# An encoder on one core: the latents' second projections in the order queries, keys, values, and the last MLP group's squares and differences placed behind part of the down projection

## The chip, the cores and the metric

The kernel runs on one core of one Trainium2 chip. A core has five engines with a queue each: TensorE (PE) for matrix products, VectorE (DVE), ScalarE (ACT) and GpSimd (POOL) for work on elements, and SyncE (SP), which here does nothing but issue loads and stores. Each engine runs its queue in order and waits on semaphores for the others. The metric is the device time of one execution in microseconds. Three runs of the kernel before took 2659.59, 2660.11 and 2661.64 us; the median, 2660.11, is the time that is predicted against.

## The reference

Two layers, 1024 tokens, width 1024, all in fp32. Each layer runs four attention groups side by side on one input projection, adds their output projection to `x`, and then an MLP with a squared ReLU:

```python
for l in range(DEPTH):
    h = rms_norm(x, norm1_g[l])
    proj = h @ w_in[l]
    ...
    y_a = mla_mixer(a_cq, a_ckv, a_kr, mla_q_norm_g[l], mla_w_uq[l], mla_kv_norm_g[l],
                    mla_w_uk[l], mla_w_uv[l], cos32, sin32)
    ...
    mix = jnp.concatenate([rms_norm(y_a, out_g_mla[l]), y_b,
                           rms_norm(y_c, out_g_swa[l]), rms_norm(y_d, out_g_na[l])], axis=-1)
    x = x + mix @ w_out[l]
    h = rms_norm(x, norm2_g[l])
    x = x + jnp.square(jax.nn.relu(h @ w_up[l])) @ w_down[l]
return rms_norm(x, final_norm_g)
```

Group A (`mla_mixer`) makes its queries, keys and values out of latents, by a second projection:

```python
q = (rms_norm(cq, q_norm_g) @ w_uq).reshape(B, S, MLA_HEADS, MLA_NOPE_DIM + MLA_ROPE_DIM)
q = jnp.concatenate([q[..., :MLA_NOPE_DIM], apply_rope(q[..., MLA_NOPE_DIM:], cos, sin)], axis=-1)
c = rms_norm(ckv, kv_norm_g)
k_nope = (c @ w_uk).reshape(B, S, MLA_HEADS, MLA_NOPE_DIM)
v = (c @ w_uv).reshape(B, S, MLA_HEADS, MLA_V_DIM)
```

## The kernel before

**Products.** Data stand transposed in SBUF: 128 features on the partitions, 1024 tokens along a row, worked on in halves of 512. An fp32 operand is cut into a rounded part and the rest (`split`, L191: ACT copies the rounded part, L195, DVE or POOL subtracts it, L189), and a product is three passes over these parts (`passes`, L221 to L223). A product therefore waits for ACT's copy and for the subtraction: `far` is an operand of the activations (rest on DVE), `wh` and `wl` are the two parts of a weight (rest on POOL in most of the MLP).

**Attention.** `weave` interleaves the heads of one group with a generator of other work (`fill`). While group D runs (`attn_d`, L492), the fill is the rest of group C's projection and then `latent_up` (L740): it loads the parts of the query latent (rank 192, so one tile of 128 rows and one of 64, stored twice) and of the key and value latent (rank 128), each as rounded part and rest (`latp`), the row factors of the norms (`rq`, `rkv`), and makes, half by half, four kinds of result: values, keys without rotation (two tiles of two heads each), queries without rotation (two such tiles) and the rotated query part. Each result is scaled, split and stored to DRAM (`va`, `kan`, `qan`, `qar`); group A's heads load it later into stacks. Between D and A lies group C (`attn_c`), whose fill holds the sums of the output projection (`sum`, loaded from x).

**MLP.** Both products are done with a seven-product scheme on 2 by 2 blocks. `mlp_up` (L1226) runs 16 groups `q`; each gives four blocks of hidden units (`p1`, `b21`, `u3`, `u2`). A block is rectified and scaled on DVE (L1256), squared on ACT (L1258) and stored to `acts` (`keep`, L1262); four differences of the squared blocks (`differ`, L1311) are stored as well, since down needs them as operands: `acts[q, 1]` to `acts[q, 7]`.

`mlp_down` (L1442) runs four parts `j`, each over four groups of hidden units and seven products, in the order 1, 2, 6, 7, 4, 5, 3. Product `o` loads `acts[4 * j + k, o]` for k = 0 to 3 (`op`, L1464), splits them (`far`), and adds each result to `x`. Products 1, 6, 7 and 4 of a part use the same four PSUM banks `u`, so PE may start block m of product 7 only when DVE has done the add of block m of product 6. The combinations of down's weights (L1495 to L1497, `raw<-raw`) run on DVE too.

**The order.** Inside the MLP PE's order is that of the code (`manual_schedule`, L1188). DVE, ACT, POOL and SP are ordered by a list scheduler. `tc.issue_after(ins)` holds back what is written in it behind `ins`, on the engine of `ins` and nowhere else.

**The last group.** At the end of `mlp_up`, group 15 still has its rectifying, squares, stores and differences to do. They are left in `self.finish_up` (L1438) and done inside down: its first entry, which is `done4` and `done3` (L1298, L1307), behind the last rounding of product 1 of j = 0 (L1481); its second, `differ`, is written at j = 1 ahead of product 6 (L1499) and tied to nothing. The loop of product 2 and of the weights' combinations in j = 0 is tied behind `self.rectified` (L1489), the last rectify that was written, so here that of `u2`. Group 15's results are read by j = 3.

## Time and profile before

| | us |
|---|---|
| median of three runs (lowest, highest) | 2660.11 (2659.59, 2661.64) |
| the profiled execution | 2666.08 |
| its span, from the first to the last instruction | 2664.3 |
| PE busy in the span | 2529.8 |
| DVE busy | 1950.1 |
| ACT busy | 1442.6 |
| POOL busy | 1127.8 |

The mean granted PE clock of the profiled execution is 0.971 of full speed. In the profile an instruction is named by line, engine, operation and tiles, `out<-in`, with the tiles' names of the program and the buffers' numbers left out: `x<-u` is an add of a product in bank `u` to x, `ev<-ev` a difference or a sum in the hidden blocks' buffers, `far<-act,far` the rest of an activation operand, `wl<-raw,wh` the rest of a weight. What stands in brackets is the idle time of the engine ahead of an instruction and what ended it. A window gives, for a stretch of the span, each engine's busy time and number of instructions, the granted clock and the share of the DMA engines' time that was in use.

### The profile page before, as it was taken

The numbers are of one execution on the slowest core, as the hardware profiler recorded it, in microseconds if no ns is written. First come the engines' busy times: TensorE is split into PE (matmuls) and PEld (weight loads), VectorE is DVE, ScalarE is ACT, GpSimd is POOL, SyncE is SP. The second block draws the span as 40 slices with busy tenths as digits, with TensorE's granted clock in tenths as the row PEclk, the third lists the DMA queues.
The fourth block names the chain that finished last, engine by engine and source line by source line (L and its number), as shares of the span: only waits on it lengthen the run. The fifth ranks groups of instructions, "written<-read, shape, count | busy, mean of one in ns | idle before, by whom it ended". The sixth has DMA issues, their size and how long they took to land.

```text
span 2664.3 us, 37498 instructions
## 1 busy us (share of the span) xinstructions
PE 2529.8 (95%) x12320; PEld 2105.1 (79%) x12320; DVE 1950.1 (73%) x3403; ACT 1442.6 (54%) x2612; POOL 1127.8 (42%) x800
## 2 busy tenths in 40 slices
PE   8899988999999998999999999889999999999998
PEld 7678877887788886888877788777877888878886
DVE  6677767784986668887568777677849866688876
ACT  4577756663644444444436777666735444444445
POOL 2465633211055554454425656332011555555554
PEclk9889998999999999999998999989999999999999
DMA  5634598331244456444245445963221544664431
GB/s 167 181 89 127 145 266 252 106 92 36 76 162 150 152 189 240 145 140 143 93 120 150 117 134 145 291 199 90 84 71 32 187 154 150 228 215 149 129 119 64
DMA packets 191539, 385.00 MB, mean 145 GB/s; under 512 B 23712, under 2 KB 34928, under 8 KB 191344
## 3 DMA queue, kind: packets, MB, share of 16 engines
q1 hardware_dynamic: 176976, 356.90, 44.2%
q10 hardware_dynamic: 14368, 25.70, 2.8%
q8 instruction: 98, 1.61, 0.3%
q14 instruction: 97, 0.79, 0.1%
HBM read 261.20 MB, written 121.32 MB: 144 GB/s over the span
## 4 chain that ended last, share of the span: by engine, by line
PE 73%; DVE 11%; DMA 7%; ACT 4%; issue 3%; POOL 1%; SPq 1%; DVEq 0%; POOLq 0%; ACTq 0%
PE u L221 8%; PE u L223 8%; PE u L222 8%; PE mm L221 5%; PE p L223 5%; PE p L221 5%; PE p L222 5%; PE mm L222 5%; PE mm L223 5%; PE sb L856 3%; DVE p L858 3%; PE tr L892 2%; DVE part L189 2%; ACT p L861 1%; PE pv L881 1%
## 5 line engine op out<-in xcount | busy, mean ns | idle before, releaser
L189 POOL TENSOR_TENSOR wl<-raw,wh 128x512 fp32r<-128x512 f32 x424 | 605.6, 1430 | 698.9 <-ACT wh L195 675.0
L195 ACT ACTIVATE wh<-raw 128x512 fp32r<-128x512 f32 x448 | 281.3, 629 | 578.3 <-PE u L222 311.4
L189 POOL TENSOR_TENSOR wl<-ws,wh 128x512 fp32r<-128x512 f32 (+1 forms) x120 | 151.1, 1261 | 451.1 <-ACT wh L195 444.2
L221 PE MATMUL u<-far,wh 128*128 128x512 f32 x768 | 301.1, 392 | 11.4 <-DVE x L189 9.2
L223 PE MATMUL u<-far,wl 128*128 128x512 f32 x768 | 300.9, 392 | 6.7 <-POOL wl L189 6.7
L222 PE MATMUL u<-far,wh 128*128 128x512 f32 x768 | 300.7, 392 | 0.0
L189 DVE TENSOR_TENSOR raw<-raw 128x512 f32<-128x512 f32 x256 | 224.9, 886 | 79.4 <-DMA raw<-in_w_up 43.1
L189 DVE TENSOR_TENSOR ptl<-tr,pth 128x512 fp32r<-128x512 f32 (+2 forms) x384 | 237.8, 628 | 60.5 <-ACT pth L195 59.4
L861 ACT ACTIVATE p<-p,nm 128x1024 f32<-128x1024 f32 x192 | 220.1, 1147 | 79.0 <-DVE nm L858 77.2
L195 ACT ACTIVATE pth<-tr 128x512 fp32r<-128x512 f32 (+2 forms) x384 | 206.0, 547 | 99.7 <-PE tr L892 63.6
L223 PE MATMUL p<-far,wl 128*128 128x512 f32 (+1 forms) x648 | 251.0, 387 | 4.0 <-DVE wl L189 4.0
L221 PE MATMUL p<-far,wh 128*128 128x512 f32 (+1 forms) x648 | 251.3, 388 | 0.0
L222 PE MATMUL p<-far,wh 128*128 128x512 f32 (+1 forms) x648 | 250.9, 387 | 0.0
L856 PE MATMUL sb<-stack 96*128 96x512 f32 x640 | 223.2, 430 | 13.9 <-DVE nm L858 12.9
L189 DVE TENSOR_TENSOR far<-act,far 128x512 fp32r<-128x512 f32 x224 | 206.1, 949 | 14.6 <-ACT far L195 14.6
L189 POOL TENSOR_TENSOR p<-p 128x1024 f32<-128x1024 f32 x64 | 154.8, 2419 | 106.3 <-ACT p L944 99.5
L221 PEld LDWEIGHTS u<-far,wh 128*128 128x128 f32 x768 | 145.1, 189 | 43.3 <-issue 10.0
L223 PEld LDWEIGHTS u<-far,wl 128*128 128x128 f32 x768 | 145.3, 189 | 37.9 <-POOL wl L189 7.8
L222 PEld LDWEIGHTS u<-far,wh 128*128 128x128 f32 x768 | 145.2, 189 | 31.0 <-DVE far L189 0.8
L221 PE MATMUL mm<-xh,wh 128*128 128x512 f32 x416 | 166.8, 401 | 1.8 <-DVE part L189 1.6
L892 PE MATMUL tr<-ident,p 128*128 128x128 f32 x1024 | 162.1, 280 | 6.3 <-DVE ptl L189 5.4
L858 DVE CUSTOM_DVE_ANT_0 p<-sb,zero 128x512 f32<-128x512 f32 x192 | 129.3, 685 | 49.5 <-PE sb L856 22.1
(255 smaller groups left out, 6150.7 us busy)
## 6 DMA issues: line engine op xcount, KB each, us to landing
act<-acts SPq DMA_DIRECT2D x224, 256.0 KB
raw<-in_w_up SPq DMA_DIRECT2D x128, 256.0 KB
acts<-ev SPq DMA_DIRECT2D x128, 256.0 KB
raw<-in_w_down SPq DMA_DIRECT2D x128, 256.0 KB
acts<-ev ACTq DMA_DIRECT2D x96, 256.0 KB
ws<-in_w_in SPq DMA_DIRECT2D x76, 256.0 KB
rz<-drows SPq DMA_DIRECT2D x40, 256.0 KB
stack<-kd SPq DMA_DIRECT2D x32, 256.0 KB
```

What stands on the lines that cost most here:

```text
L189: return (eng or self.nc.vector).tensor_tensor(out=out, in0=a, in1=b, op=op)
L195: self.rounded = nc.scalar.activation(hi, src, AF.Copy)
L221: mm(ps, w[0], x[0][:, sl], start=start, stop=False)
L222: mm(ps, w[0], x[1][:, sl], start=False, stop=False)
L223: mm(ps, w[1], x[0][:, sl], start=False, stop=stop)
L856: self.nc.tensor.matmul(ps, q[:, qt * P:(qt + 1) * P], k[:, sl], start=i == 0, stop=i == len(passes) - 1)
L858: self.nc.vector.tensor_tensor_reduce(out=p[:, sl], in0=ps, in1=self.zero[:, 0:1].bitcast(F).broadcast_to([P, 512]), scale=-scale, scalar= ...
L861: self.nc.scalar.activation(p, p, AF.Exp, bias=nm[:, 1:2], scale=-1.0, accum_out=z)
L881: nc.tensor.matmul(out, v[:, kt], lo[:, sl], start=False, stop=kt == 7)
L892: nc.tensor.transpose(t[:, k * 256 + i * P:k * 256 + (i + 1) * P], p[:, (j * 2 + k) * P:(j * 2 + k + 1) * P], self.ident)
```

## The change

Two functions' order changes; what is computed stays the same.

In `latent_up` the loads and the projections change places. The row factors are loaded first, then the query latents, then the key and value latent. The projections run: rotated queries, queries of the first two heads, keys of the first two heads, values, queries of the last two, keys of the last two. Before they ran: values, keys, queries of the last two heads, rotated queries, queries of the first two.

In the MLP the last group's work is parted otherwise. Behind product 1's rounding in j = 0 stand only the rectify of `b21`, which frees its bank, and the add to `u2`, which frees the other. The square and the store of `b21`, the rectifies, squares and stores of `u3` and `u2`, and `differ` stand at j = 1 and are tied behind the last add of j = 1's product 1. `self.rectified` is thereby `b21`'s rectify when j = 0's loop is tied to it.

```diff
@@ latent_up
-        def latent(i, r):
+        rq, rkv = self.big_tile(F, "rq"), self.big_tile(F, "rkv")
+        self.spread(rq, rows[0])
+        self.spread(rkv, rows[1])
+        parts = []
+        for i, r in ((0, P), (1, 64), (2, P)):
             p = []
             for j in range(2):
                 t = self.big_tile(R, "latp")
                 for at in range(0, P, r):
                     self.load(t.bitcast(F)[at:at + r], lat[j, i, :r])
                 p.append(t)
-            return tuple(p)
-
-        rkv = self.big_tile(F, "rkv")
-        kv = latent(2, P)
-        self.spread(rkv, rows[1])
-        q = [latent(0, P), latent(1, 64)]
-        rq = self.big_tile(F, "rq")
-        self.spread(rq, rows[0])
+            parts.append(tuple(p))
...
+        w0 = self.weights(d["w_lat"][l, 0])
+        yield from two([w0[0], both(w0[1])], parts[0:2], self.ev_rope(tabs, qr))
         plain = lambda r, dst: self.ev_plain(r, self.to_parts(dst))
+        yield from two([w0[2], both(w0[3])], parts[0:2], plain(rq, qn[:, 0]))
+        w1 = self.weights(d["w_lat"][l, 1])
+        yield from two(w1[2:3], parts[2:3], plain(rkv, kn[:, 0]))
         w2 = self.weights(d["w_lat"][l, 2])
         for t in range(2):
-            yield from two(w2[t:t + 1], [kv], self.ev_plain(rkv, self.to_values(va[2 * t:2 * t + 2])))
-        w1 = self.weights(d["w_lat"][l, 1])
-        for t in range(2):
-            yield from two(w1[2 + t:3 + t], [kv], plain(rkv, kn[:, t]))
-        yield from two([w1[0], both(w1[1])], q, plain(rq, qn[:, 1]))
-        w0 = self.weights(d["w_lat"][l, 0])
-        yield from two([w0[0], both(w0[1])], q, self.ev_rope(tabs, qr))
-        yield from two([w0[2], both(w0[3])], q, plain(rq, qn[:, 0]))
+            yield from two(w2[t:t + 1], parts[2:3], self.ev_plain(rkv, self.to_values(va[2 * t:2 * t + 2])))
+        yield from two([w1[0], both(w1[1])], parts[0:2], plain(rq, qn[:, 1]))
+        yield from two(w1[3:4], parts[2:3], plain(rkv, kn[:, 1]))
@@ mlp_up
             def relu2(v, src, n):
 
+                rectify(v, src, n)
+                nc.scalar.activation(v, v, AF.Square)
+                return v
+
+            def rectify(v, src, n):
                 self.rectified = nc.vector.scalar_tensor_tensor(out=v, in0=src, scalar=0.0, in1=rb[:, N[n]],
                                                                 op0=ALU.max, op1=ALU.mult)
-                nc.scalar.activation(v, v, AF.Square)
-                return v
...
-            self.finish_up = [lambda: (done4(s), done3(s)), lambda: differ(s)]
+
+            def free():
+                s.b21 = tmp()
+                rectify(s.b21, s.u, 0)
+                self.tt(s.u2, s.p, s.u2, ALU.add)
+
+            def rest():
+                nc.scalar.activation(s.b21, s.b21, AF.Square)
+                keep(s.q, 2, s.b21)
+                relu2(s.u3, s.u3, 1)
+                keep(s.q, 3, s.u3)
+                relu2(s.u2, s.u2, 1)
+                differ(s)
+
+            self.finish_up = [free, rest]
@@ mlp_down
-                self.tt(o, ps, o, ALU.add)
+                return self.tt(o, ps, o, ALU.add)
...
-                        add(m, 0, u[m])
+                        added = add(m, 0, u[m])
...
                 if j == 1:
-                    self.finish_up[1]()
+                    with tc.issue_after(added.ins):
+                        self.finish_up[1]()
```

How the orders differ, at three places. On DVE, layer 0, at the passage from up into down, the program before runs as follows, from the eight operand rests of product 1 of j = 0 onwards:

```order
L189 TENSOR_TENSOR far<-act,far 128x512 x8
L1256 SCALAR_TENSOR_TENSOR ev<-ev,rb 128x512
L1256 SCALAR_TENSOR_TENSOR ev<-u,rb 128x512
L189 TENSOR_TENSOR ev<-p,ev 128x512
L189 TENSOR_TENSOR far<-act,far 128x512
L1256 SCALAR_TENSOR_TENSOR ev<-ev,rb 128x512
L189 TENSOR_TENSOR raw<-raw 128x512 x4
L189 TENSOR_TENSOR far<-act,far 128x512 x3
```

and the changed program, at the same place:

```order
L189 TENSOR_TENSOR far<-act,far 128x512 x8
L1258 SCALAR_TENSOR_TENSOR ev<-u,rb 128x512
L189 TENSOR_TENSOR raw<-raw 128x512 x4
L189 TENSOR_TENSOR ev<-p,ev 128x512
L189 TENSOR_TENSOR raw<-raw 128x512
L189 TENSOR_TENSOR far<-act,far 128x512
```

The two rectifies `ev<-ev,rb` (of u3 and u2) are gone from here, and the weights' combinations `raw<-raw` follow the first rectify at once. A little later, still in j = 0, the program before has the four differences among the adds of product 1 and the operands of products 6 and 7; here the last of product 1's adds with its neighbours:

```order
L189 TENSOR_TENSOR x_7183<-u,x_7183 128x512
L189 TENSOR_TENSOR far<-act,far 128x512
L189 TENSOR_TENSOR raw<-raw 128x512
L189 TENSOR_TENSOR far<-act,far 128x512
L189 TENSOR_TENSOR ev<-ev 128x512 x2
L189 TENSOR_TENSOR x_7190<-u,x_7190 128x512
```

and the changed program:

```order
L189 TENSOR_TENSOR x_7183<-u,x_7183 128x512
L189 TENSOR_TENSOR far<-act,far 128x512
L189 TENSOR_TENSOR raw<-raw 128x512
L189 TENSOR_TENSOR far<-act,far 128x512
L189 TENSOR_TENSOR x_7190<-u,x_7190 128x512
L189 TENSOR_TENSOR far<-act,far 128x512 x2
```

No difference `ev<-ev` is left in j = 0. In j = 1, on DVE as well, the changed program has them behind the last add of product 1:

```order
L189 TENSOR_TENSOR x_7190<-u,x_7190 128x512
L1258 SCALAR_TENSOR_TENSOR ev<-ev,rb 128x512 x2
L189 TENSOR_TENSOR far<-act,far 128x512 x2
L189 TENSOR_TENSOR raw<-raw 128x512
L189 TENSOR_TENSOR x_7169<-p,x_7169 128x512
L189 TENSOR_TENSOR ev<-ev 128x512
L189 TENSOR_TENSOR raw<-raw 128x512
L189 TENSOR_TENSOR x_7176<-p,x_7176 128x512
L189 TENSOR_TENSOR ev<-ev 128x512 x3
L189 TENSOR_TENSOR x_7183<-p,x_7183 128x512
```

The two rectifies stand ahead of the last two operand rests of product 6, the differences among the adds of product 2. On SP, layer 0, around `latent_up`'s loads (a piece of the difference, - before, + changed; `bias` and `kd` belong to group D, `in_w_lat` are the second projections' weights):

```order
 L160 DMA rz<-drows 64x1024
 L160 DMA v<-vd 128x1024
-L160 DMA latp<-lat 128x1024 x2
+L160 DMA rq<-drows 128x1024
 L160 DMA rkv<-drows 128x1024
 L160 DMA latp<-lat 128x1024 x2
 L160 DMA latp<-lat 64x1024 x4
-L160 DMA rq<-drows 128x1024
+L160 DMA latp<-lat 128x1024 x2
 L160 DMA ws<-in_w_out 128x256
 L160 DMA stack<-kd 64x1024 x2
 L160 DMA stack<-kc 64x1024
```

The first latent load stands behind two loads of row factors of 512 KB now; what comes after the group is as it was, the load of `bias` at its row included. Further on, the four loads `sum<-in_x` stand behind the first eight stack loads of group A, where before they stood ahead of all but one of them.

## The prediction

> **What bounds the kernel now.** I read the page's busy times and its chain first, then the table of windows, the waits of PE inside the windows that are not full, and last the timelines of DVE, PE and POOL there.
>
> ```profile
> PE 2529.8 (95%) x12320; PEld 2105.1 (79%) x12320; DVE 1950.1 (73%) x3403; ACT 1442.6 (54%) x2612; POOL 1127.8 (42%) x800
> PE 73%; DVE 11%; DMA 7%; ACT 4%; issue 3%; POOL 1%; SPq 1%; DVEq 0%; POOLq 0%; ACTq 0%
> ```
>
> PE bounds nearly everything: only 2664.3 − 2529.8 = 134.5 us of the span are without a matmul. The change leaves the number and kind of matmuls alone, so it can only move those 134.5 us and what PE loses at a lower clock. The windows show where (window, length, then busy time of PE, PEld, DVE, ACT and POOL with counts, granted PE clock, DMA share, GB/s):
>
> ```profile
> 356.00:400.00 44.00, 35.73 (x202) 30.68 (x200) 28.42 (x73) 26.40 (x69) 11.63 (x10) 0.92 0.98 280
> 1000.00:1060.00 60.00, 49.05 (x203) 38.83 (x202) 56.32 (x69) 28.16 (x50) 26.50 (x17) 0.92 0.68 236
> 1060.00:1335.00 275.00, 275.00 (x1215) 227.73 (x1214) 196.19 (x238) 121.37 (x194) 136.13 (x100) 1.00 0.42 134
> 1670.00:1700.00 30.00, 26.30 (x159) 23.15 (x157) 16.75 (x40) 16.83 (x41) 9.09 (x5) 0.94 1.04 291
> 2310.00:2370.00 60.00, 52.87 (x220) 42.71 (x219) 50.32 (x64) 30.42 (x53) 32.10 (x18) 0.91 0.77 267
> ```
>
> The rest of down (1060 to 1335) has no idle PE at all. The two passages from up into down (1000 to 1060 in layer 0, 2310 to 2370 in layer 1) lose 10.95 and 7.13 us, DVE being busy 56.32 of 60 us in the first. The two stretches in which `latent_up` runs (356 to 400, 1670 to 1700) lose 8.27 and 3.70 us, with the DMA engines full. So the change touches four places that lose about 30 us together; nothing else can pay.
>
> The waits of PE in the two passages (what waits, for whom: total, times, longest):
>
> ```profile
> PE u L221 <- DVE x L189: 9.2, 2, 7.6
> PE u L223 <- POOL wl L189: 0.6, 1, 0.6
> ...
> PE u L223 <- POOL wl L189: 6.0, 1, 6.0
> ```
>
> The first two rows are layer 0, the last is layer 1. They are different cases: layer 0 waits for DVE, layer 1 for one POOL operation.
>
> **Part 1: the last group's operations, layer 0.** DVE in the passage (start, duration, line, operation, count; the number in brackets, where there is one, is idle time before it), then PE around the long wait:
>
> ```profile
> 1012.94 1.77 DVE L1256 SCALAR_TENSOR_TENSOR ev<-ev,rb 128x512 f32<-128x512 f32 x1
> 1016.43 0.68 DVE L1256 SCALAR_TENSOR_TENSOR ev<-ev,rb 128x512 f32<-128x512 f32 x1
> 1030.37 0.68 DVE L189 TENSOR_TENSOR far<-act,far 128x512 fp32r<-128x512 f32 x1
> 1030.97 0.68 DVE L189 TENSOR_TENSOR x<-u,x 128x512 f32<-128x512 f32 x1
> 1032.77 0.68 DVE L189 TENSOR_TENSOR ev<-ev 128x512 f32<-128x512 f32 x1
> 1040.64 3.48 DVE L189 TENSOR_TENSOR ev<-ev 128x512 f32<-128x512 f32 x2
> 1048.73 1.75 DVE L189 TENSOR_TENSOR ev<-ev 128x512 f32<-128x512 f32 x1
> 1054.61 1.87 DVE L189 TENSOR_TENSOR x<-u,x 128x512 f32<-128x512 f32 x3
> ...
> 1047.46 0.39 PE L223 MATMUL u<-far,wl 128*128 128x512 f32 x1
> 1055.43 0.77 PE L221 MATMUL u<-far,wh 128*128 128x512 f32 x1 [7.58 <-DVE x L189]
> 1055.99 0.63 PE L222 MATMUL u<-far,wh 128*128 128x512 f32 x1
> 1060.24 0.40 PE L223 MATMUL u<-far,wl 128*128 128x512 f32 x1
> ```
>
> From 1012.94 DVE runs without a gap until the first of three adds at 1054.61, and that add (done about 1055.3) lets PE start product 7 at 1055.43. The six operations in the five rows of L1256 and ev<-ev are those that the change takes out of this stretch: two rectifies and four differences. All others stay, among them the rectify of b21 and the add ev<-p.
>
> As recorded the six take 1.77 + 0.68 + 0.68 + 3.48 + 1.75 = 8.36 us. That is not what removing them must give. The rows at 1030.37 and 1030.97 show operations following each other every 0.60 us; others take 1.7. The window from 1012.94 to the add's end says why:
>
> ```profile
> 1012.94:1055.28 42.34, 32.62 (x141) 25.66 (x139) 42.34 (x51) 20.00 (x35) 20.58 (x13) 0.94 0.54 179
> 1038.40 5.17 POOL L189 TENSOR_TENSOR wl<-raw,wh 128x512 fp32r<-128x512 f32 x3 [0.54 <-ACT wh L195]
> ```
>
> By the timeline 49 DVE operations begin in it and end by 1055.3 (the 51 adds one cut at either edge). 49 at 0.60 are 29.4 us; the 12.9 us over them match the 13 POOL operations at about 1.0 each (the row of three shows their length, 1.7): DVE and POOL take turns, and each turn of POOL costs whichever DVE operation is next. The POOL operations all stay. So 43 operations and 13 turns take 25.8 + 12.9 = 38.7 us, a gain of **6 × 0.60 = 3.6 us**; the upper end is 8.4 as recorded. I take 3.6, since all 13 turns remain and only their partners change.
>
> The Trainium skill bears on this choice: "SBUF — State Buffer", section "SBUF: two separate sides", says that VectorE with two SBUF inputs and GpSimd share one pair of ports as an exclusive lock held for a whole instruction. By that rule a removed instruction that had waited hands its wait to the next one, which gives the 3.6; were the long durations the instructions' own, the sum would be 8.4. The rows at 0.60 and 1.7 for one shape agree with the rule.
>
> What is late next: PE ended product 6 at 1047.46 + 0.39 = 1047.85, with two shorter waits before it (9.2 − 7.6 = 1.6 for DVE, 0.6 for POOL), so it can be ready at 1045.6 if those go. DVE's add comes at 1055.4 − 3.6 = 1051.8. A wait of about 6 us stays, as does the slow start behind it: from 1055.99 to 1060.24 ten matmuls come every 0.43 us, against 0.23 before (1047.46 and its neighbours), which costs 12 × 0.2 = 2.4 us. Layer 0 gains **3.6**.
>
> ACT: one square now sits among the copies of product 6's operands, two later ones are gone from there; at 0.6 us each beside an ACT busy 28.16 of 60 us they cost nothing; uncovered, 0.6. SP's four stores of the differences leave the queue of the operand loads, which then wait for nothing but their own buffers: nothing below zero counted. POOL's own queue is not changed.
>
> **Layer 1.** POOL at the place of the 6.0 us wait, DVE's operation that ends it, and PE:
>
> ```profile
> 2340.28 10.71 POOL L189 TENSOR_TENSOR wl<-raw,wh 128x512 fp32r<-128x512 f32 x3 [5.17 <-ACT wh L195]
> ...
> 2346.41 0.68 DVE L189 TENSOR_TENSOR x<-u,x 128x512 f32<-128x512 f32 x1
> 2372.43 1.87 DVE L189 TENSOR_TENSOR x<-u,x 128x512 f32<-128x512 f32 x3
> ...
> 2347.67 0.79 PE L223 MATMUL u<-far,wl 128*128 128x512 f32 x1 [6.04 <-POOL wl L189]
> 2353.80 0.43 PE L222 MATMUL p<-far,wh 128*128 128x512 f32 x1
> 2375.43 0.39 PE L221 MATMUL u<-far,wh 128*128 128x512 f32 x1
> ```
>
> Here one POOL operation, begun at 2340.28, ended only when DVE came to an add that reads PSUM at 2346.41; until then DVE's operations followed each other unhindered. PE lost 6.0 us, then 15 matmuls at 0.43 (up to 2353.80) another 3.0. It began product 7 at 2375.43 with no wait for DVE, whose add was done at 2373.05. If POOL is held up in the same way again, fewer DVE operations later help nobody: gain 0. If not, PE is ready at 2375.4 − 9.0 = 2366.4, and DVE, which now gives way to about three more POOL turns at 1.0 and has six operations fewer at 0.60, at 2373.05 + 3.0 − 3.6 = 2372.4; a wait of 6.0 and a slow start of 2.4 follow, and the matmuls behind it stand at 2374.9: gain 0.5. I take **0** for layer 1. The upper end is 8.4: the same six at recorded lengths (6.2) and no hold-up, 2375.4 less 2367.0. A new hold-up in layer 0 would cost 9.0 there, bring PE to product 7 at 1054.6 and remove the wait for DVE and its slow start: still 3.2 gained.
>
> **Where the six go: second part, j = 1.** DVE ahead of its product 6 and 7, and PE's first matmul of product 6:
>
> ```profile
> 1117.99 0.68 DVE L189 TENSOR_TENSOR raw<-raw 128x512 f32<-128x512 f32 x1
> 1126.17 0.68 DVE L189 TENSOR_TENSOR x<-u,x 128x512 f32<-128x512 f32 x1
> ...
> 1123.05 0.39 PE L221 MATMUL u<-far,wh 128*128 128x512 f32 x1
> ```
>
> Two rectifies now stand ahead of the last two operand pieces of product 6, which were ready at 1117.99, 5.1 us before PE wanted them; at 0.60 to 1.7 each they cost 1.2 to 3.4. All six stand ahead of product 7's last piece, ready at 1126.2; PE begins product 7 48 matmuls after 1123.05, at about 1134.0, so 7.8 us are free against 3.6 to 10.2. Cost **0** in both layers (nearest row: the mean of the six as recorded, 1.4, makes 8.4, of which only 0.6 would show, and that in the last piece); uncovered, 2.4 a layer. Behind the tied operations on DVE queue only these operands and adds. The three squares and six stores that land here meet a PE without idle time and DMA engines 42% busy; the stores are wanted by j = 3.
>
> **Part 2: `latent_up`.** No instruction is added or removed, so the price is one of order alone. PE at the first latent product and at the next long wait, DVE's wait behind that, then the sums:
>
> ```profile
> 367.94 0.47 PE L221 MATMUL mm<-latp,wh 128*128 128x512 f32 x1 [2.24 <-DMA latp<-lat]
> 369.13 0.50 PE L222 MATMUL mm<-latp,wh 128*128 128x512 f32 x1 [0.72 <-DMA latp<-lat]
> 387.72 1.62 PE L1026 MATMUL sb<-stack 128*128 128x384 f32 x4 [4.05 <-DVE nb L1102]
> DVE p L1102 <- DMA bias<-in_bias: 4.5, 1, 4.5
> 448.98 1.29 DVE L189 TENSOR_TENSOR sum<-mm,sum 128x512 f32<-128x512 f32 x2 [3.59 <-DMA sum<-in_x]
> PE sb L1026 <- DVE nb L1133: 4.5, 1, 4.5
> PE sb L1026 <- DVE nb L1133: 1.8, 1, 1.8
> ```
>
> The first product already waits for its loads, and two loads of 512 KB (rq, rkv) now stand ahead of them on SP. The two halves landed 1.2 us apart (367.94, 369.13), so the first product comes 2.4 later. It is now a query product, which also needs the four 256 KB loads behind: by the same pace another 2.4, of which the other matmuls that the order puts between hide some. PE is then 2.4 to 4.8 late; but at 387.72 it waited 4.05 for the bias load, which stands at the same row of SP behind the same bytes, so it lands as before and swallows about as much. Net 0 in layer 0; uncovered 4.8. Layer 1 has no such later load in its trace; the window from 1670 has 3.7 idle in all. Its ends are 0 and 4.8.
>
> The sums (loads of x for the output product) are issued behind the first stacks of group A rather than ahead, and DVE's adds stand later too. In before, DVE waited 3.6 for one and kept PE waiting 4.5 (layer 0), and 1.8 at the like place in layer 1. Ends: minus 6.3 if the later adds no longer wait, plus the like if the loads slip further than the adds. With costs of both signs and nearly equal ends I take **0** for all of attention.
>
> **Sum.** 3.6 + 0 + 0 + 0. The profiled execution took 2666.08, 6 us over the median 2660.11 of the runs; a difference of 3.6 (0.14%) carries over unchanged: 2660.1 − 3.6 = **2656.5**. About 0.2%, 5.3 us, is what a measurement here can tell from no change, so the forecast itself is on the edge of "same".
>
> **Rivals.**
> - Recorded lengths count (17%): the six take their 8.4 with them in layer 0. Then DVE's add comes at 1047.0, PE waits 1.4 instead of 7.6, and the slow start goes too: 8.4 + 2.4 = 10.8, 2649.3. For: 8.36 stood in the trace. Against: the sum of 0.60s and turns fits without them. The trace has no slow start behind the 1.6 us wait and one behind 6.0 and 7.6, so a short rest would spare the 2.4. The Trainium skill, "TensorE: Matmul & The Clock Gate", "What's actually happening", puts that limit at an idle window of about 3.4 us; by it the wait of 6 that I leave stays above, as the rows have it.
> - The sums stop blocking DVE (17%): 3.6 + 4.5 + 1.8 = 9.9, 2650.2. For: the adds stand later. Against: so do the loads.
> - Slower, the latents come late (20%): the 4.8 of the query product shows in both layers, 9.6 − 3.6 = +6.0, 2666.1. It decides once PE's delay exceeds the 4.05 of the bias wait, or if SP, waiting for PE to free stack buffers, issues the bias that much later. For: DMA shares of 0.98 and 1.04 there. Against: the cover in layer 0, and in layer 1 a DMA queue that PE did not wait for as long.
> - The moved work is not hidden (8%): 2.4 a layer in j = 1 gives back 4.8: 2661.3. Against: 7.8 us of room.
> - It does not do what it says (10%): layer 0 finds another last wait, POOL or a load, and stays at 2660.
>
> **Chances.** The forecast holds 28%, with its own range 2653 to 2659, of which a quarter (7%) lies under 2654.8. Faster: 17 + 17 + 7 = 41%. Slower: 20%. Within 0.2%: 21 + 8 + 10 = 39%. The range reaches from under the two fast rivals to over the slow one, 2646 to 2667; both fast ones together (2643) and 4.8 uncovered with j = 1 on top stay outside.
>
> **What would show it.** In the profile after: DVE's first add of product 6 in j = 0 some 38.7 us after its first rectify; a wait for DVE of about 6 us ahead of product 7 and ten matmuls at 0.43 behind it; in layer 1 either the same hold-up of POOL or a wait for DVE in its place; no idle PE in j = 1; the first latent matmul near 370, and the wait for the bias shorter by what that one grew. Wrong would be: a wait ahead of product 7 under 3 us, idle PE after 1060, or windows of `latent_up` more than 2 us longer or shorter.

## The result, and the profile after

The changed kernel takes 2643.61 us (median of six runs, 2638.36 to 2649.87); before, taken in the same session, 2658.05 (six runs, 2653.90 to 2661.64). The ratio is 0.9946, with a 95% interval of 0.9928 to 0.9963: 14.4 us faster, where 3.6 had been forecast, and outside the range. The profiled execution took 2649.87, its span is 2648.1; it is the longest of the six, and stands 16.2 below the profiled one of before, which at 2666.08 is itself longer than each of the six timed ones. So two profiles show where the time went, and the timings how much.

The busy times and the chain of the page of after:

```profile
PE 2524.9 (95%) x12320; PEld 2097.0 (79%) x12320; DVE 1950.6 (74%) x3403; ACT 1443.9 (55%) x2612; POOL 1134.4 (43%) x800
PE 74%; DVE 10%; DMA 6%; ACT 4%; issue 3%; POOL 2%; SPq 1%; DVEq 0%; POOLq 0%; ACTq 0%
```

The counts are those of before. PE is busy 4.9 us less (the same matmuls, at a mean granted clock of 0.975 instead of 0.971) and idle 11.3 less: 2648.1 − 2524.9 = 123.2 against 134.5.

To see where, I cut the executions at the same counts of matmuls. From the 1700th to the 2350th the kernels run the same matmuls in another order, and from the 7400th to the 8450th the same but for four. Cuts inside these two stretches don't part equal work, because the order differs. Counting the columns of each matmul (512 for a 128x512), those from 8000 to 8450 have 137,616 before and 131,600 after, and those from 7800 to 8000 have 54,048 and 57,248; in layer 0, from 1950 to 2350, the two kernels are within 0.4%. Stage lengths in us, from one profiled execution each:

| stage (cut at PE's matmuls) | before | after | after, profiled again |
|---|---|---|---|
| layer 0, latents and C, no. 1700 to 3400 | 334.8 | 328.8 | 324.7 |
| of which D gives way to C, 1950 to 2350 | 90.1 | 85.4 | 80.9 |
| layer 0, 1700 to 2350 (the same matmuls) | 142.8 | 136.4 | 132.6 |
| layer 0, passage up to down (420 matmuls) | 109.9 | 105.9 | 104.6 |
| layer 1, latents and C, 7800 to 9530 | 342.2 | 337.1 | 331.7 |
| of which the first latent products, 7800 to 8000 | 40.2 | 44.1 | 40.9 |
| of which D gives way to C, 8000 to 8450 | 102.9 | 94.7 | 92.9 |
| layer 1, 7400 to 8450 (the same but for four) | 217.7 | 213.7 | 208.6 |
| layer 1, passage up to down (420 matmuls) | 105.9 | 105.1 | 105.7 |

The two executions of the changed kernel differ by up to 5.4 us in a row, and those of another kernel below (the latents alone) by 10 in the first row, so single us mean nothing here. Still, against this one profile of before the attention gives 11 to 21 us, the MLP about 5. Part of that belongs to this profile: three kernels below that have the old `latent_up` as well take 332.2 to 334.3 us in the first row and 338.3 to 340.1 in layer 1's. I call the 400 matmuls (layer 0) and 450 (layer 1) in which group D's last heads, the last latent projections and group C's first heads mix **the turn**. Its windows, before (columns as in the prediction: PE, PEld, DVE, ACT, POOL, granted clock, DMA share, GB/s):

```profile
410.65:500.74 90.09, 75.73 (x401) 64.61 (x400) 66.24 (x165) 57.80 (x145) 32.40 (x29) 0.91 0.67 194
1711.20:1814.13 102.93, 88.37 (x452) 74.52 (x451) 76.64 (x194) 67.92 (x177) 37.44 (x33) 0.88 0.72 205
```

and after, with two windows of down behind product 6 of j = 0:

```profile
406.91:492.28 85.37, 75.28 (x402) 61.71 (x401) 62.75 (x162) 56.30 (x144) 24.55 (x25) 0.94 0.69 208
1704.44:1799.11 94.67, 83.05 (x452) 69.13 (x451) 72.63 (x186) 66.98 (x171) 28.25 (x27) 0.93 0.72 216
1040.00:1310.00 270.00, 270.00 (x1193) 223.65 (x1192) 195.94 (x241) 114.62 (x189) 134.45 (x100) 1.00 0.42 135
2350.00:2620.00 270.00, 270.00 (x1193) 223.65 (x1192) 204.83 (x253) 126.81 (x212) 135.71 (x99) 1.00 0.40 125
```

PE is idle in layer 0's turn for 10.1 us instead of 14.4, and in layer 1's for 11.6 instead of 14.6. There PE is also busy for 83.1 us instead of 88.4, but with 4.4% fewer columns, so most of that difference is work that now stands ahead of the cut. On the same matmuls layer 1 gains 4.0 and 9.1 us in the two profiles, not the 8.3 and 10.0 of the turn. In down PE is busy for every one of 540 us: the work that was moved into j = 1 is hidden.

What stood in the turn before, on DVE. Three of its groups by line in the first 44 us of layer 0's (count, busy time, mean ns of one, idle time ahead of them and what ended it):

```profile
L189 DVE TENSOR_TENSOR part<-mm,tabs 64x512 f32<-64x512 f32 x4 | 2.8, 689 | 0.1
L189 DVE TENSOR_TENSOR part<-mm,rq 128x512 f32<-128x512 f32 x3 | 2.1, 685 | 1.5 <-PE tr L1035 1.2 <-POOL both L189 0.3
L189 DVE TENSOR_TENSOR part<-mm,tabc 128x512 f32<-128x512 f32 x2 | 1.4, 681 | 0.0
```

Two rows of layer 1's timeline:

```profile
1720.38 0.69 DVE L189 TENSOR_TENSOR part<-mm,rq 128x512 f32<-128x512 f32 x1 [3.56 <-POOL both L189]
1723.17 0.68 DVE L189 TENSOR_TENSOR part<-mm,tabc 128x512 f32<-128x512 f32 x1
```

And DVE's two longest waits in the first 70 us of layer 1's turn (in total, times, longest):

```profile
DVE p L1133 <- PE tr L1035: 3.9, 2, 2.6
DVE part L189 <- POOL both L189: 3.6, 1, 3.6
```

The tabs and tabc rows are the rotated queries: three DVE and two POOL operations (`part`, `both`) for each half, all in the turn. In layer 1 DVE could not start a query's evacuation for 3.56 us, because POOL had not finished with an earlier one, and group D's and C's softmax stood in the same queue. In layer 0 the same wait is 0.3 us (the second row above), so it is not what layer 0 gained by. In after the rows of tabs and tabc are gone from both turns, and so is the wait; there stand, beside a query and a key projection, the values, whose evacuation has no POOL operation.

The passages: waits of PE, after, in layer 0 and then in layer 1:

```profile
PE u L223 <- POOL wl L189: 6.1, 1, 6.1
PE u L221 <- ACT ev L1292: 1.2, 1, 1.2
...
PE u L223 <- POOL wl L189: 6.7, 1, 6.7
PE u L221 <- ACT ev L1292: 1.1, 1, 1.1
```

and the timeline of POOL, DVE and PE in layer 0's:

```profile
1011.43 11.20 POOL L189 TENSOR_TENSOR wl<-raw,wh 128x512 fp32r<-128x512 f32 x3 [4.69 <-ACT wh L195]
1016.83 1.29 DVE L189 TENSOR_TENSOR far<-act,far 128x512 fp32r<-128x512 f32 x2
1018.04 0.69 DVE L189 TENSOR_TENSOR x<-u,x 128x512 f32<-128x512 f32 x1
1019.30 0.80 PE L223 MATMUL u<-far,wl 128*128 128x512 f32 x1 [6.05 <-POOL wl L189]
1024.59 0.63 PE L223 MATMUL p<-far,wl 128*128 128x512 f32 x1
1040.97 0.69 DVE L189 TENSOR_TENSOR x<-u,x 128x512 f32<-128x512 f32 x1 [1.84 <-PE u L223]
```

Layer 0 now has the hold-up that only layer 1 had: POOL's first operation begins at 1011.43 and alone takes 7.82 us, DVE's follow each other every 0.60 us, and POOL gets through when DVE comes to an add that reads PSUM, at 1018.04. PE waits 6.05 and then runs 12 matmuls at 0.43. In return it no longer waits 7.58 for DVE ahead of product 7; at 1040.97 DVE waits for PE.

### The profile page after: what moved, and what is told of

Read it like the earlier page. It is cut to its first block, busy times and chain, and to the rows that moved or that the text cites. A ratio compares the mean times of both kernels' runs of the same rounds, so it can differ in the third digit from the quotient of the medians.

```text
span 2648.1 us, 37521 instructions
## 1 busy us (share of the span) xinstructions
PE 2524.9 (95%) x12320; PEld 2097.0 (79%) x12320; DVE 1950.6 (74%) x3403; ACT 1443.9 (55%) x2612; POOL 1134.4 (43%) x800
## 4 chain that ended last, share of the span: by engine, by line
PE 74%; DVE 10%; DMA 6%; ACT 4%; issue 3%; POOL 2%; SPq 1%; DVEq 0%; POOLq 0%; ACTq 0%
PE u L221 9%; PE u L223 9%; PE u L222 8%; PE p L223 5%; PE p L221 5%; PE p L222 5%; PE mm L221 5%; PE mm L222 5%; PE mm L223 5%; PE sb L853 3%; PE tr L889 2%; DVE p L855 2%; DVE part L189 2%; DMA bias<-in_bias 2%; ACT p L858 1%
## 5 line engine op out<-in xcount | busy, mean ns | idle before, releaser
L189 POOL TENSOR_TENSOR wl<-raw,wh 128x512 fp32r<-128x512 f32 x424 | 611.9, 1444 | 688.9 <-ACT wh L195 671.4
L195 ACT ACTIVATE pth<-tr 128x512 fp32r<-128x512 f32 (+2 forms) x384 | 206.9, 548 | 100.5 <-PE tr L889 68.4
L853 PE MATMUL sb<-stack 96*128 96x512 f32 x640 | 220.0, 426 | 15.7 <-DVE nm L855 15.1
L223 PEld LDWEIGHTS u<-far,wl 128*128 128x128 f32 x768 | 145.1, 189 | 43.7 <-POOL wl L189 13.6
```

What stands on the lines that cost most here:

```text
L189: return (eng or self.nc.vector).tensor_tensor(out=out, in0=a, in1=b, op=op)
L195: self.rounded = nc.scalar.activation(hi, src, AF.Copy)
L223: mm(ps, w[1], x[0][:, sl], start=False, stop=stop)
L853: self.nc.tensor.matmul(ps, q[:, qt * P:(qt + 1) * P], k[:, sl], start=i == 0, stop=i == len(passes) - 1)
```

## The experiments

All ratios are against the kernel before on the same chip, with their 95% intervals. "Turn" gives the lengths between the same counts of matmuls as above, layer 0 and layer 1. Since these cuts don't part equal work in layer 1, here are for all profiles the two stretches that do, in us (in layer 1 at most five of the 1050 matmuls differ):

| kernel | layer 0, 1700 to 2350 | layer 1, 7400 to 8450 |
|---|---|---|
| old `latent_up`: before; MLP alone; differences alone; adds, old `latent_up` | 142.8; 142.8; 140.6; 140.7 | 217.7; 214.2; 216.3; 215.3 |
| new `latent_up`, both parts changed (two profiles) | 136.4; 132.6 | 213.7; 208.6 |
| new `latent_up`, the latents alone (two profiles) | 136.7; 129.3 | 205.8; 205.8 |
| new `latent_up` with the adds (two profiles) | 132.7; 131.8 | 203.0; 206.7 |
| new projections, old loads | 137.5 | 215.9 |
| rotated queries last | 143.5 | 212.9 |
| rotated queries first, the rest in the old order | 137.8 | 216.7 |
| values last; the same with the adds | 142.3; 141.6 | 216.3; 216.2 |
| factors first | 145.1 | 219.4 |
| POOL's operations on DVE | 146.3 | 219.6 |

**Each half alone.** `latent_up` changed and the MLP as before; then the MLP changed and `latent_up` as before.

> Only latent_up is changed; the MLP is as before. Theory A (the larger part of the gain is attention's: set against each other by the number of the matmul, the two profiles part by 6.4 us in layer 0 and by about 4 us in layer 1 between the start of latent_up and the end of group C): 8 to 12 us under the kernel before. Theory M (the gain is the MLP's, and attention's part of it is chance of the two profiled executions): within 3 us. Both: the passages from up into down are as before, 7.6 us of waiting for DVE in layer 0 and 6.0 for POOL in layer 1.

> Only the MLP is changed; latent_up is as before. Theory A: 4 to 6 us under the kernel before (4.1 in layer 0 and 0.9 in layer 1 by the two profiles), with a wait of about 6 us for one POOL operation in both layers and no wait for DVE. Theory M: 11 to 15 us.

The latents alone: 2649.62, 0.9946 [0.9926, 0.9965]; a second time 2647.07, 0.9948 [0.9931, 0.9966]. The MLP alone: 2654.85, 0.9977 [0.9965, 0.9990], which is 6.1 us with ends of 2.7 and 9.3. The turn in the first two executions of the latents alone:

```profile
410.13:494.26 84.13, 74.25 (x402) 61.97 (x401) 63.23 (x162) 56.36 (x144) 24.84 (x25) 0.94 0.71 211
1710.66:1799.41 88.75, 79.75 (x453) 64.97 (x451) 74.70 (x189) 66.64 (x174) 28.26 (x27) 0.98 0.77 234
```

```profile
403.03:483.31 80.28, 71.37 (x402) 59.00 (x401) 63.34 (x162) 56.22 (x144) 24.98 (x25) 0.98 0.71 221
1693.60:1784.44 90.84, 82.13 (x452) 67.77 (x451) 75.57 (x189) 66.98 (x174) 28.25 (x27) 0.94 0.76 230
```

So the part that I priced at nothing is worth about 14 us by the ratios (11.5 and 14.5 by the medians), and is there in both layers of both profiles. The code of the MLP is that of before here, but its passages are not: 110.0 and 109.4 us, the second time 109.4 and 110.9, against 109.9 and 105.9 before. PE's wait for DVE in layer 0's and layer 1's:

```profile
PE u L221 <- DVE x L189: 9.2, 1, 9.2
...
PE u L221 <- DVE x L189: 9.1, 1, 9.1
```

Beside the changed latents, then, the MLP's part gives 3.5 to 5.8 us in each layer's passage (105.9, 104.6 and 105.1, 105.7 in the changed kernel); beside the old ones it gives 3.7 and 1.1.

PE's waits in the two passages of the MLP alone:

```profile
PE u L221 <- DVE x L189: 5.5, 1, 5.5
PE u L221 <- ACT ev L1295: 1.1, 1, 1.1
PE u L221 <- ACT wh L195: 0.8, 1, 0.8
```

These three rows are the same in both layers. This is the forecast's own picture, a wait for DVE of about 6 with slow matmuls behind it (12 and 5), and no hold-up of POOL. In layer 0 DVE is done with the add that ends the wait 38.2 us after it began the first rectify; 38.7 had been forecast. Passages 106.2 and 104.9.

**Only the differences moved.** Before, with `differ` tied behind j = 1's add of product 1, and nothing else.

```diff
-                        add(m, 0, u[m])
+                        added = add(m, 0, u[m])
...
-                    self.finish_up[1]()
+                    with tc.issue_after(added.ins):
+                        self.finish_up[1]()
```

> The kernel before, with the four differences alone tied behind the add of j = 1; rectifies, squares and latent_up as before. At 0.60 an operation DVE's add ahead of product 7 in layer 0 comes 2.4 us earlier, at recorded lengths 5.9, which would end the slow matmuls as well (8). By the first, 2 to 3 us under the kernel before; by the second 6 to 9; if POOL is held up in layer 0 too, the wait of 7.6 for DVE goes and one of 6 for POOL comes, 3 to 4 us.

2653.45, 0.9980 [0.9966, 0.9995]; passages 106.7 and 106.7; PE waits 5.5 and 5.6 for DVE, and 2.1 and 1.8 for POOL. The time cannot be told from that of the whole MLP part. In layer 0's passage the four differences alone bring 3.2 of the 3.7 us, the rectifies and squares little; in layer 1's they bring nothing.

**Loads or projections?** The row factors first, projections as before; then the new projections, each row factor behind its latents.

> latent_up as before but for one thing: the loads of the row factors rq and rkv are issued ahead of the latents; projections in the old order, MLP as before. Theory F (the row factors came late: DVE's queue stood 3.7 us behind the wait for rkv and POOL's 12.1 us behind the one for rq): it has most of a1's gain, 5 to 10 us under before. Theory O (the order of the projections matters, by what they store and what is loaded behind them): within 3 us of before, or slower by up to 3, since the first latent lands later.

> latent_up with the projections in the new order, but each row factor's load behind its own latents, as before; MLP as before. Theory F: within 3 us of before, and DVE or POOL wait for rq or rkv as before. Theory O: 7 to 11 us under before.

Factors first: 2666.97, 1.0019 [1.0005, 1.0033], turn 96.1 and 105.1. New projections alone: 2655.96, 0.9979 [0.9966, 0.9992], turn 85.2 and 96.8. In before DVE waited 3.7 us for rkv and POOL 12.1 for rq, and I had taken an earlier landing for a possible cause. In the first kernel this row stands among POOL's waits:

```profile
POOL tabc L189 <- DMA rq<-drows: 0.5, 1, 0.5
```

and the time is longer all the same. An early row factor by itself pays nothing; the order of the projections shortens layer 0's stretch (in layer 1, 215.9 on the same matmuls is a length of the old order), and with the loads ahead of it (the latents alone, 14 us) pays more than without (5 us).

**Rotated queries last.** The changed kernel, with that one projection at the end, beside the changed kernel itself.

```diff
-        yield from two([w0[0], both(w0[1])], parts[0:2], self.ev_rope(tabs, qr))
...
         yield from two(w1[3:4], parts[2:3], plain(rkv, kn[:, 1]))
+        w0 = self.weights(d["w_lat"][l, 0])
+        yield from two([w0[0], both(w0[1])], parts[0:2], self.ev_rope(tabs, qr))
```

> The changed kernel once more, beside the others of this call. If the parts simply add (14 us for latent_up alone, 6 for the MLP alone), 20 us under the kernel before; if, as the first timing has it, the two get in each other's way, 12 to 16. The orders that the scheduler writes say the second: in layer 0 the changed kernel and latent_up alone have one order, in layer 1's attention they have two.

> The changed kernel with one thing undone: the rotated queries' projection comes last in latent_up, all else as changed. Theory R (what pays is that the rotated queries' evacuation, six operations on DVE and two on POOL for each result, no longer falls on the turn from group D to group C, but into the stretch before it that waits for DMA): the turn in layer 0, 170 matmuls, goes from 37 us back to 41 to 44, POOL's operations in it from 12 to 15 or more, and the kernel is 5 to 12 us slower than the changed one. Theory L (the loads' order, or queries ahead of keys as such): the turn stays at 36 to 38, the total within 3 us of the changed kernel.

The changed kernel: 2641.04, 0.9931 [0.9911, 0.9950], turn 80.9 and 92.9. With the rotated queries last: 2652.44, 0.9966 [0.9953, 0.9978]; the turn's windows:

```profile
409.96:498.93 88.97, 75.20 (x401) 62.57 (x400) 66.16 (x167) 57.17 (x147) 28.80 (x28) 0.94 0.63 191
1701.61:1801.19 99.58, 84.36 (x451) 68.20 (x451) 75.27 (x190) 66.91 (x175) 33.20 (x31) 0.95 0.70 216
```

8.1 and 6.7 us longer than in the changed kernel beside it, and 11.4 in the time: this one projection undoes the attention part, or nearly. On the same matmuls layer 0 shows it (143.5 against 136.4 and 132.6). In layer 1, 212.9 lies between the changed kernel's 213.7 and 208.6, so for that layer it is not shown. And what came back is not the wait for POOL: with the rotated queries in the turn again, DVE waits for `both` in neither layer. It waits for the loads of the sums, and PE behind it; layer 0, then layer 1:

```profile
DVE sum L189 <- DMA sum<-in_x: 3.8, 1, 3.8
PE mm L279 <- DVE sum L189: 4.4, 1, 4.4
...
DVE sum L189 <- DMA sum<-saved: 3.8, 1, 3.8
PE sb L1024 <- DVE nb L1131: 4.0, 3, 3.4
```

In the changed kernel beside it DVE waits 1.0 for the sums in layer 0 and not at all in layer 1, and PE has no wait behind them.

**Rotated queries first, nothing else.** MLP as before, loads as changed, then rotated queries, values, keys, both queries (the first weights are loaded and split twice).

> MLP as before. latent_up with its loads as changed, the rotated queries first, then the old order (values, keys, the other queries); the first weight tile is loaded and split a second time for that. Theory P (the turn from group D to C is as long as POOL's operations in it make it, since each costs DVE about 1 us; the rotated queries' four are what the old order adds there): POOL's operations in layer 0's turn fall from 15 to about 11 or 12, the turn from 43 to 44 us to 36 to 39. Theory V (it is the values, which need no POOL, standing at the turn in the new order): 15 or more operations and 42 to 45 us.

2660.51, 0.9994 [0.9983, 1.0004]. Its turn:

```profile
408.11:493.25 85.14, 75.02 (x401) 63.17 (x400) 65.19 (x161) 57.26 (x147) 31.04 (x29) 0.92 0.71 209
1705.67:1804.92 99.25, 83.94 (x450) 67.46 (x451) 73.96 (x191) 67.99 (x179) 32.17 (x29) 0.95 0.69 209
```

In layer 0's turn that is enough (85.1, as after; 137.8 on the same matmuls), in layer 1's it is not (99.3; 216.7). The time shows no gain of either: the interval leaves at most 4.5 us, and what the second load and split of the weights cost is not parted from it. The next two show what it isn't.

**POOL's operations on DVE.** Before, with what `latent_up`'s evacuations do on POOL done on DVE.

```diff
+                eng, self.eng = self.eng, nc.vector
                 ev(n, ps)
+                self.eng = eng
```

> The kernel before, except that the second projections' evacuations do on DVE what they did on POOL (12 subtractions and additions a layer); order, loads and MLP as before. Theory P: the turn has POOL's operations down from 15 to 7 to 10, and although DVE has as many more of its own at 0.6 us, it gets 2 to 4 us shorter in layer 0 (39 to 42). Theory W (it is the evacuations' work at the turn that counts, on whichever engine): as long as before or up to 4 us longer, 43 to 48.

2668.81, 1.0031 [1.0020, 1.0042].

```profile
406.15:501.05 94.90, 78.46 (x401) 63.20 (x400) 73.51 (x174) 57.93 (x146) 21.70 (x20) 0.93 0.62 181
1707.24:1811.32 104.08, 87.99 (x451) 72.37 (x451) 80.81 (x205) 68.18 (x177) 22.02 (x21) 0.92 0.71 202
```

POOL does 20 operations there instead of 29, DVE nine more, and the turn is longer. The count of POOL's operations doesn't set it: the kernel above it has 29 in layer 0, and a short turn there.

**Values last.** Rotated queries, queries and keys of the first two heads, then of the last two, and the values at the end, so that what stands in the turn passes through no POOL operation; with the MLP as before, and with the MLP of the fastest kernel, below.

> latent_up with the changed loads and the projections rotated queries, queries of the first two, keys of the first two, queries of the last two, keys of the last two, values; MLP as before. So the last projections, which run while groups D and C change places, are the ones whose evacuation has no POOL operation, and all ten POOL operations per half-pair of queries and keys lie earlier. Theory Q (what counts at the turn is whether DVE and PE stand behind evacuations that pass through POOL): turn from D to C 37 to 38 us in layer 0 and no longer than 57.5 us in layer 1 (the latent-only kernel had 37.9 and 57.5), DVE waiting nowhere in it for POOL's both; time 2645 to 2651, as the latent-only kernel's 2649.6 or better. Rival (only the rotated queries count, whatever else stands at the turn): the same turns, no gain over the latent-only kernel, and no loss. Rival (values at the turn are worse, since their evacuation puts transposes on PE's queue and 512 KB stores in the way of group A's first loads): layer 1's turn over 60 us, or group A's start late; time over 2653.

2661.47, 0.9999 [0.9987, 1.0010].

```profile
408.65:499.35 90.70, 77.81 (x402) 62.70 (x401) 66.34 (x162) 54.49 (x141) 22.29 (x23) 0.91 0.65 190
1708.90:1809.42 100.52, 84.42 (x452) 71.36 (x452) 73.63 (x189) 66.20 (x173) 27.90 (x27) 0.90 0.70 204
```

My theory fell: POOL has 22.3 us of work in layer 0's turn, less than in after, and the gain is gone, on the same matmuls too (142.3 and 216.3). The first 170 matmuls of the turn take 36.9 us, as in after (37.0), but the rest 53.8 instead of 48.4. The values come with transposes on PE, which the other results don't have.

**Product 1's adds among the combinations.** The changed kernel holds DVE on weights' combinations and operands while POOL waits. Here block m's combinations, m = 1 to 3, are tied behind the add of block m − 1, so that an add from PSUM comes sooner and more often.

```diff
-                        added = add(m, 0, u[m])
+                        adds.append(add(m, 0, u[m]))
...
-                        self.tt(s1[m], a21[m], a22[m], ALU.add)
-                        sub(a21[m], a11[m], a21[m])
-                        sub(a11[m], s1[m], a11[m])
+                        with ExitStack() as turn:
+                            if j == 0 and m:
+                                turn.enter_context(tc.issue_after(adds[m - 1].ins))
+                            self.tt(s1[m], a21[m], a22[m], ALU.add)
+                            sub(a21[m], a11[m], a21[m])
+                            sub(a11[m], s1[m], a11[m])
```

> The changed kernel, and in j = 0 the weights' combinations of block m = 1 to 3 are tied behind the add of product 1's block m - 1, so that DVE reads PSUM every few operations while POOL makes product 1's weights. Theory H (in both layers a POOL operation is held up by DVE's unbroken row of 14 operations on two SBUF operands, and PE's wait of 6 us and the slow matmuls behind it come from that): PE's wait for POOL falls from 6 to under 2.5, no slow matmuls, and after a new short wait for DVE at product 7 each passage is 3 to 6 us shorter; total 6 to 12 under the changed kernel. Rival (the POOL operation was late for another reason, its input or its own length): the wait stays near 6.

> The MLP of t1 with latent_up as before. If t1's 6 us over the changed kernel came from layer 1's attention, whose order in t1 is that of latent_up alone, and not from the passages (105.1 us in t1, 104.6 to 105.9 in the changed kernel), this one lies within 3 us of the MLP change alone, 2652 to 2656 with the kernel before at 2659; if t1's ties pay in the MLP, 5 us or more below that.

> The order with the values last, with the fastest kernel's MLP (last group's work parted as changed, combinations tied between the adds). If the latents' order and the MLP's ties add up, the time is v1's minus what the ties gave over the latent-only kernel (2649.6 to 2635 across calls, 14.5): 2631 to 2637. If the combination depends on the order that the scheduler then finds in layer 1's attention, the second passages stay at 105 and the stretch of layer 1's latents differs from v1's by over 4 us either way.

With both parts of the change: **2634.65**, 0.9900 [0.9880, 0.9921], and again 2635.74, 0.9904 [0.9891, 0.9918]: the fastest kernel here, 25 us under before. With the old `latent_up`: 2644.39, 0.9940 [0.9926, 0.9955]. With the values last: 2649.91, 0.9961 [0.9947, 0.9975]. PE's waits in the first one's layer 0 passage, of 105.1 us:

```profile
PE u L221 <- DVE x L189: 3.7, 1, 3.7
PE u L221 <- ACT wh L195: 1.2, 1, 1.2
PE u L221 <- ACT ev L1292: 1.1, 1, 1.1
PE u L223 <- POOL wl L189: 0.9, 1, 0.9
```

and in the one with the old `latent_up`, alike in both layers, passages of 100.5 us each:

```profile
PE u L221 <- DVE x L189: 2.0, 1, 2.0
PE u L223 <- POOL wl L189: 1.2, 1, 1.2
PE u L221 <- ACT ev L1295: 1.1, 1, 1.1
```

The hold-up is gone in both. In the first one's layer 0 it was not a PSUM add that let POOL through: the operation that had taken 7.82 us takes 1.40 there, from 1008.05, while the first add comes at 1013.32. A wait for DVE of 3.7 has come in the hold-up's place, with slow matmuls behind it, so the passage is no shorter than after's; in the second that wait is 2.0, and not one matmul of the passage runs at 0.43. The code of the MLP is the same: with the changed `latent_up` the scheduler puts three of the last operand rests (`far`) ahead of the first add, with the old one five. What the first one gains over after, it gains in layer 1's attention, 325.5 and 327.8 us against 337.1 and 331.7; the order of PE's and of POOL's instructions is that of the latents alone, one for one, while after's has another matmul at 1301 places of PE's list, all between the 6594th and the 8461st, in layer 1 ahead of its MLP.

## Why the prediction was wrong

**The step that failed** is the last of part 2: "I take **0** for all of attention", with the rule ahead of it, that PE's lateness at the first latent product and the sums are what the order of `latent_up` can move. The term is about −14 us (ends 9 and 20), by the latents alone. I priced the two ends of the stretch, its loads and the sums, let the one pay for the other, and never asked which projections stand at its end. The profile had the place: before's two turns have 14.4 and 14.6 us without a matmul, more than any window that the prediction shows, and the rows of tabs and tabc stood in their timeline. The prediction's table jumps from 400.00 to 1000.00 and from 1700.00 to 2310.00. The first stretches that it leaves out, 400.00 to 490.00 and 1700.00 to 1805.00, have 13.6 and 15.7 us without a matmul, and they stood in the fuller table of windows that I had. So "four places that lose about 30 us together; nothing else can pay" was wrong by my own numbers.

**Layer 0's passage: right in size, by another road.** Forecast 3.6; measured 4.0 (109.9 to 105.9), and 5.3 in the second profile. The mechanism that I took for likeliest, 43 operations at 0.60 and 13 turns of POOL, then a wait of 6, is what the MLP alone showed, with 38.2 us where 38.7 was forecast, a wait of 5.5 in place of 7.6 and a passage 3.7 shorter. In the changed kernel the clause at the end of layer 1's step came true instead, "A new hold-up in layer 0" with "still 3.2 gained"; that both roads come to nearly the same gain is luck.

**Layer 1's passage.** Forecast 0; measured −0.9 and −0.2 in the changed kernel, and −1.1 with the MLP alone. The hold-up of 6.0 came back as 6.7, as the step allowed. What the step left out is that the new `latent_up` changes this passage as well: with the old MLP it is 3.5 and 4.9 longer than before's, so the forecast of nothing came out as the sum of that loss and of a gain of about the same size.

**j = 1.** Forecast 0, in both layers; PE has no idle time there. Right.

**The first latent products.** "PE is then 2.4 to 4.8 late": in layer 0 they began at 367.40, which counted from the 1700th matmul is 1.6 later than before, and 2.2 in the second profile; the wait behind the bias is down from 4.05 to 0.49, as forecast. In layer 1 the stretch is longer by 3.9 in one profile and 0.7 in the other, but it holds 5.9% more columns. The first latent product begins 1.9 and 1.3 later there, counted from the 7800th matmul, after a wait of 4.4 and 4.9 for DVE (1.7 before) and not for a load. So the slower rival, late latents, is not what layer 1 shows.

**The rivals.** Recorded lengths count: fell, for with the six gone PE still waits 5.5 ahead of product 7 where that rival had 1.4. The sums: in part. PE's wait of 4.5 behind them in layer 0 is 2.8 in after and gone in its second profile, and the 1.8 in layer 1 is gone or nearly gone in both, which is 3 to 6 us of the 6.3; with the rotated queries last both are back, as 4.4 and 3.4. It is not the whole: with the factors first PE has no such wait in layer 0 either, and that stretch is longer than before's. The moved work: hidden. None of the five held the whole cause, and the range's lower end, 2646, was set by them.

**What stays open.** Shown is where the gain is made, in `latent_up`'s stretch of the attention, and that the place of the rotated queries matters: moved to the end alone, they cost 11.4 us. Put first alone, they shorten layer 0's stretch in one profile, but the time shows no gain. What else is needed isn't settled, nor by what road it works. In layer 0 the wait for POOL isn't it (0.3 us), and where the rotated queries stand last there is none in either layer; the wait for the sums returned there, but as an effect of the order or as a cause is not parted. POOL's count (20 operations and a long turn, 29 and a short one) and freedom from POOL (values last) are both refuted as rules, and neither rotated queries nor values may come last. I also could not part the waits from the granted clock, which in layer 1's turn rose from 0.88 to 0.93: no run holds the one and moves the other.

The two halves alone give about 14 and 6 us. Together they gave 14.4 (ends 9.8 and 19.1) and 18.3 (ends 13.3 and 23.7), so it isn't even certain that they fail to add up. The profiles show two ways in which each half reaches into the other: with the MLP's part layer 1's attention (7800 to 9530) takes 337.1 and 331.7 us, against 328.5 and 328.6 without it, in another order of PE's matmuls; and the new latents make layer 1's passage of the old MLP 3.5 and 4.9 longer, which the MLP's part takes back.

## What to carry to other kernels

Where projections are woven into attention, look at the stretch in which they end as closely as at that in which they begin: which result is made last there was worth 11 us here, and no simple count of operations told which one it should be. Try the orders, and do not expect that one projection moved alone brings the gain: put first alone, the rotated queries brought nothing in the time. Cut two executions at equal counts of matmuls before explaining anything: the table shows at once which stage moved, and how much is noise. Check that the cuts part equal work, though; here one of them did not, and made 8.3 us out of a gain of 4.0. And where a list scheduler orders the engines, a tie in one part can reorder a part far away, so each half of a change has to be measured by itself.

## What the runs showed of the hardware

- A POOL operation that elsewhere in the passage took 1.3 to 1.8 us took 7.82 and 8.28 in layer 0 and layer 1 of the changed kernel, while DVE's operations on SBUF followed each other every 0.60 us; it ended about 1.2 us after DVE began an add that reads PSUM (1018.04 and 2331.65). With the combinations tied between the adds PE's wait for POOL was 0.9 to 1.2 us instead of 6.1 and 6.7. That the add is what lets POOL through is not shown: in one of these kernels the operation took 1.40 us with no such add near it.
- In the passages, waits of PE of 3.7 us and more were followed by 5 to 13 matmuls at 0.43 us instead of 0.23. In the kernel without a slow matmul (adds, old `latent_up`) the longest wait was 2.0. One passage (values last, adds among the combinations, layer 0) had seven slow ones a few matmuls behind two waits close together, the longer 1.3 us, so the length of a single wait is not the whole rule.
- Taking the evacuations off POOL made the kernel slower by 8 us (1.0031). DVE had nine operations more in layer 0's turn; whether that is why is not shown.
